# A decoder layer in fp32 pieces on one core: attention's product with the values from the last key block to the first, and the gating unit's scaling one tick later

## The chip, the cores and the metric

One core of a Trainium2 chip runs the whole layer as one program. The metric is device time of one execution in microseconds (us); lower is better. Engines are named as the profile names them: PE multiplies matrices, PEld loads PE's stationary operand, ACT and DVE work on elements, POOL does a little of that and issues some DMAs, SP issues the other DMAs.

## The reference, cut to what matters

One layer of a hybrid decoder: 512 tokens, width 2048. One projection gives the operands of two branches, a spatial gating unit and stick-breaking attention, whose merged result goes on into a feed-forward part and a per-layer embedding. The change lies in two places of the branches: the product of the attention weights with the values, and the norm of the gating unit's values.

```python
h = rmsnorm(x, attn_norm_g);  proj = h @ w_in        # u | v_sgu | q | k | v_att | g_a | g_b
...
v_sgu = rmsnorm(gelu(v_sgu).reshape(B, S, 8, 128), sgu_norm_g)
mixed = einsum('gts,bnsgc->bntgc', tril(w_s), v_sgu in chunks of 128) + b_s
y_a   = gelu(u) * mixed                              # gating unit
...
z      = einsum('bhqd,bhkd->bhqk', rmsnorm(q), rmsnorm(k)) * 128 ** -0.5    # 8 heads of 128
strict = key_pos < q_pos
log_1m = where(strict, log_sigmoid(-z), 0)
tail   = cumsum(log_1m, reverse=True) - log_1m       # sum over the keys behind this one
w      = where(strict, exp(log_sigmoid(z) + tail), 0)
y_b    = einsum('bhqk,bhkd->bhqd', w, v_att)         # <- the change's first part
...
x += (sigmoid(g_a) * (y_a @ w_up_a) + sigmoid(g_b) * (y_b @ w_up_b)) @ w_o
x += SwiGLU(rmsnorm(x));  x += sigmoid(rmsnorm(x) @ w_pg) * (p @ w_ple)
```

## The kernel before

**The large products.** The weights stream through the core in units: SP loads a unit into `wholes`, POOL issues a second load that adds onto it (L361), DVE adds two blocks (L373), and each unit is split into a high part on ACT (L357, into `whi`) and a low part on DVE (L354, into `wlo`), three slots of each in turn. A *pair* is one output block of 256 x 512 made of seven products of half-size blocks (a Strassen-like scheme) over eight units. Most products take three matmuls (L294, L295, L296: high by high, high by low, low by high); the first ones of many pairs, the *doubled* ones, take two (L683). When a pair's last unit is under way, its products end one after another in the `ps` banks of PSUM, and the *mix* puts them together: ACT copies halves of products out (L739), DVE adds and subtracts the others (L742). The next pair's products need the banks again, so a mix that ends late makes PE wait at the start of a product of the next pair. Two more banks of PSUM (`small`) serve everything else.

**The clock.** `tick()` is called while a pair adds its units: eight ticks a pair. Everything of the branches that is not a large product hangs on this clock: `beside(generator)` runs the generator on until its next `yield n`, and again n ticks later. So what lies between two yields is put into the instruction streams at one place among the pairs' matmuls; the engines then run their own streams in order. The scheduler may still move an instruction that is not ready in its model behind others, so that the place is not exactly that of the code; on ACT and DVE the weights' splits and the mix keep their order among each other (`in_turn`).

**Attention** runs in four rounds of two heads, between 120 and 560 us. A head has four key blocks of 128, j = 3 to 0; block j concerns the queries from block j on, (4 - j) * 128 columns. For each block, in the order j = 3, 2, 1, 0 (the `tail` is carried from behind), `stage_a` makes the scores (L1095), `stage_m` the masked logs, `stage_b` and `stage_c` split them (L1122 on ACT, L1126 on DVE), and `stage_d` makes the sums with a triangular matrix (L1132, L1133), subtracts them (L1137 on DVE) and takes the exponential (L1138 on ACT), which is the block's weights. `finish(h)` multiplies the four blocks with the values (L1145, plain fp32, which PE does as two passes) into one `small` bank, and ACT copies the result out (L1147). `finish(0)` stands after the second head's first `stage_b`, one tick behind the first head's last `stage_d`; `finish(1)` stands two ticks behind the second head's last `stage_d`.

**The gating unit** (`sgu_v`) runs in four calls of two halves, between 635 and 775 us. A half turns 512 tokens of one group over (L1021, PE), takes the squares' sums on ACT (L1028), scales and shifts them on DVE (L1193) and takes them to the power of -0.5 on POOL (L919, into `rr`). One `yield` later, ACT scales the values by `rr` (L1044, four times 128 columns; the same line serves attention's norms), and two yields later PE multiplies with the gating matrix (L1202, four matmuls of 128 columns), and DVE adds the bias (L1203).

The numbers behind names (`small_2849`) are a program's own count of buffers.

Of the kernel before, what the change touches and what calls it, by code (L numbers as in the profile page):

```python
# [19 lines left out]
P = 128  # L20
T = 512
NT = T // P
# [46 lines left out]
def hybrid_layer(  # L69
# [18 lines left out]
    nc = tc.nc  # L88
# [25 lines left out]
    class Arena:  # L114
# [28 lines left out]
        def give(self, block):  # L143
            self.turns += 1
            self.given[block.start // P : -(-(block.start + block.n) // P)] = self.turns
            holes = sorted(self.holes + [(block.start, block.n)])
            self.holes = holes[:1]
            for s, n in holes[1:]:
                if sum(self.holes[-1]) == s:
                    self.holes[-1] = (self.holes[-1][0], self.holes[-1][1] + n)  # L150
                else:
                    self.holes.append((s, n))
# [26 lines left out]
    def small_bank():  # L179
        return psa.tile([P, T], F32, tag="small", name=nm("small"))  # L180
# [333 lines left out]
    def load(src, n=1024, how="old"):  # L514
        b = take(n, how)
        nc.sync.dma_start(out=b.f(0, 1024), in_=src)
        return b
# [399 lines left out]
    def power(ms, n):  # L917
        r = rms_tile()[:, :n]
        nc.gpsimd.tensor_tensor(out=r, in0=ms, in1=expo[:, :n], op=ALU.pow)  # L919
        return r  # L920
# [90 lines left out]
    def a_tile(tag, n=T, start=0):  # L1011
        return att[tag].f(start, start + n)
# [4 lines left out]
    def flip(o):  # L1017

        ps = small_bank()
        for t in range(NT):  # L1020
            nc.tensor.transpose(ps[:, t * P : (t + 1) * P], o[:, t * P : (t + 1) * P], ident)  # L1021
        return ps

    def squares(ps):

        ms, junk = small(NT), tmp.tile([P, P], F32, tag="diag", name=nm("sq"))
        for t in range(NT):
            nc.scalar.activation(junk, ps[:, t * P : (t + 1) * P], AF.Square,  # L1028
                                 accum_out=ms[:, t : t + 1])
        return ms  # L1030
# [10 lines left out]
    def times(dst, ps, r):  # L1041
        for t in range(NT):
            s = slice(t * P, (t + 1) * P)
            nc.scalar.activation(dst[:, s], ps[:, s], AF.Copy, scale=r[:, t : t + 1])  # L1044
# [29 lines left out]
    def attention(rnd, kT, rk, v):  # L1074
        state = {}
# [64 lines left out]

        def finish(h):
            y = small_bank()
            for j in range(NT):
                c = h * T + j * P
                nc.tensor.matmul(y[:, j * P :], v[:, c : c + P], state.pop((h, "w", j)),  # L1145
                                 start=j == 0, stop=j == NT - 1)
            nc.scalar.activation(qT[:, h * T : (h + 1) * T], y, AF.Copy)  # L1147
            if h == 1:
                nc.sync.dma_start(out=y_spill[rnd], in_=qT)
                give(y_b[rnd])  # L1150
                y_done["b", rnd] = True
# [7 lines left out]
        for i, (h, j) in enumerate(blocks):  # L1159
            ahead = blocks[i + 1 : i + 3]  # L1160
            stage_b(j)
            yield 1
            if i == NT:
                finish(0)
            stage_c(j)
            if ahead:
                stage_m(*ahead[0])
            yield 1
            stage_d(h, j)
            if ahead[1:]:  # L1170
                stage_a(*ahead[1])
            yield 1
        yield 1
        finish(1)
        if rnd == 3:
            for tag in ("first", "k", "v", "zs", "zh", "zl"):
                give(att.pop(tag))

    def sgu_v(rnd, o):

        for h in range(2):
            g = 2 * rnd + h
            ws = a_tile("w2", P, rnd % 2 * P)
            nc.sync.dma_start(out=ws, in_=wsT[g])
            nc.gpsimd.affine_select(out=ws, in_=ws, pattern=[[1, P]], compare_op=ALU.is_ge,
                                    fill=0.0, base=0, channel_multiplier=-1)
            bb = a_tile("w1", P, rnd % 2 * P)
            nc.sync.dma_start(out=bb, in_=b_s[g : g + 1, :].broadcast_to([P, P]))
            yield 2
            gv = a_tile(("l", "w0")[rnd % 2])  # L1190
            ps = flip(o[:, h * T : (h + 1) * T])
            ssq = squares(ps)
            nc.vector.tensor_scalar(out=ssq, in0=ssq, scalar1=1.0 / P, scalar2=EPS,  # L1193
                                    op0=ALU.mult, op1=ALU.add)
            rr = power(ssq, NT)
            yield 1
            times(gv, ps, rr)
            yield 2
            mp = small_bank()
            for t in range(NT):  # L1200
                s = slice(t * P, (t + 1) * P)
                nc.tensor.matmul(mp[:, s], gv[:, s], ws, start=True, stop=True)  # L1202
            nc.vector.scalar_tensor_tensor(  # L1203
                out=o[:, h * T : (h + 1) * T].rearrange("p (n t) -> p n t", t=P),
                in0=mp.rearrange("p (n t) -> p n t", t=P),
                scalar=gcol[:, g_sgu + g : g_sgu + g + 1],
                in1=bb.unsqueeze(1).to_broadcast([P, NT, P]),
                op0=ALU.mult, op1=ALU.add)
# [78 lines left out]
    for n, ((w, i), pr) in enumerate(zip(order, made())):  # L1287
        if n == 0:
            row1 = norm1.row()
            for eps, c in ((eps_cols, EPS), (eps_q, EPS * P)):  # L1290
                nc.vector.tensor_scalar(out=eps, in0=norm1.mean, scalar1=c, scalar2=None,
                                        op0=ALU.mult)
        if n == 0:
            a_tiles()
        o = pr.out(block(w, i) if n < 3 else None)
        if w == "q":
            beside(q_prep(o, i))
        elif w == "k":
            kT, rk = o, rms_tile()
            beside(k_prep(kT, rk))  # L1300
            beside(attention(i, kT, rk, a_tile("v", 1024)), 6)
        elif w == "v":
            beside(v_prep(o, a_tile("v", 1024)))
        elif w == "s":
            scaled(o, row1)
            nc.scalar.activation(o, o, AF.Gelu_apprx_tanh)
            beside(sgu_v(i, o))
        elif w == "u":
            scaled(o, row1)
            nc.scalar.activation(o, o, AF.Gelu_apprx_tanh)  # L1310
            nc.vector.tensor_tensor(out=y_a[i].f(), in0=o, in1=y_a[i].f(), op=ALU.mult)
            y_done["a", i] = True
        else:
            d = tc.dram_tile([P, 1024], F32, name=nm("gsp"))
            nc.sync.dma_start(out=d, in_=o)
            gate_spill[w, i] = d
# [46 lines left out]
    for j in range(KU):  # L1363
# [10 lines left out]
        h = raw.popleft()  # L1374
# [41 lines left out]
    for c, units in enumerate(hs):  # L1416
# [3 lines left out]
        for j in range(KU):  # L1420
# [3 lines left out]
            h = load(spill["x1", j]) if end else None  # L1424
# [130 lines left out]
```

## Time and profile before

| | us |
|---|---|
| runs of the kernel (three) | 2667.51, 2673.37, 2673.16 |
| their median | 2673.16 |
| the profiled execution, its own time | 2668.2 |
| its span (first to last record) | 2666.5 |
| PE busy in the span | 2640.4 |
| DVE busy, ACT busy, POOL busy | 2236.4, 1413.9, 453.4 |
| granted TensorE clock (1 is full) | 0.998 |

The profile is one execution. The runs fall into two groups, one at 2667.5 to which the profiled execution belongs, the other 5.7 us above. "Busy" on PE includes time in which a matmul is in flight behind another. In the views, a row such as `288.98 2.39 PE L1145 MATMUL small<-wholes ... x8 [0.84 <-ACT wholes L1138]` reads: at 288.98 us PE began eight instructions of line 1145 that took 2.39 us together, and it had been idle for 0.84 us before, which ended when ACT's line 1138 had written `wholes`. fp32 matmuls are two instructions each in the trace, one for each pass.

### The profile page before, as it was taken

To read this page: it belongs to the slowest core of one execution; us is meant where nothing else is said; L and a number is where in the kernel's file an instruction comes from. 1 tells how busy PE (TensorE), PEld (TensorE's weight loads), DVE (VectorE), ACT (ScalarE), POOL (GpSimd) and SP (SyncE) were. 2 spreads that over 40 slices of the span, in tenths; PEclk is the share of its full clock that TensorE was granted. 3 is DMA by queue.
4 is the path that set the end of the run, shared out by engine and by line. 5 is a ranking of instruction groups with operands and counts; after the bars stand their busy time and mean duration, and the time that the engine had idled before them with its cause. 6 is when DMAs were issued, how large, how long until landed. Compare 5 with 4: busy or idle time off the path is not lost.

```text
span 2666.5 us, 42598 instructions
## 1 busy us (share of the span) xinstructions
PE 2640.4 (99%) x15354; PEld 2312.4 (87%) x15354; DVE 2236.4 (84%) x3791; ACT 1413.9 (53%) x2245; POOL 453.4 (17%) x557
## 2 busy tenths in 40 slices
PE   8999999999999999999999999999999999999999
PEld 7888898888998888888888888888888888889898
DVE  8687878787887658989889888888889989989876
ACT  7656565655554334576444444444445445455643
POOL 0222322222220001101111111111110211211010
PEclk9999999999999999999999999999999999999999
DMA  7577777677775669988888878888787989988884
GB/s 227 158 190 174 185 173 187 171 182 197 179 188 186 214 212 264 239 265 223 220 218 207 210 194 207 203 203 202 197 209 223 263 220 277 226 248 246 252 229 134
DMA packets 293875, 560.16 MB, mean 210 GB/s; under 512 B 26400, under 2 KB 140832, under 8 KB 293664
## 3 DMA queue, kind: packets, MB, share of 16 engines
q1 hardware_dynamic: 231408, 442.08, 50.4%
q0 software_dynamic: 62256, 115.37, 27.0%
q8 instruction: 120, 1.97, 0.3%
q14 instruction: 91, 0.75, 0.1%
HBM read 505.97 MB, written 51.38 MB: 209 GB/s over the span
## 4 chain that ended last, share of the span: by engine, by line
PE 88%; DVE 5%; ACT 2%; DMA 2%; issue 1%; POOL 0%; SPq 0%; POOLq 0%; DVEq 0%; ACTq 0%
PE ps L683 49%; PE ps L295 10%; PE ps L296 10%; PE ps L294 10%; PE small L683 6%; DVE wlo L354 2%; DVE out L742 1%; PE small L1145 1%; PE small L1021 1%; DMA wholes<-x 1%; DMA wholes<-w_in 1%; ACT whi L357 1%; DVE wholes L373 0%; PE small L1095 0%; DVE parts L285 0%
## 5 line engine op out<-in xcount | busy, mean ns | idle before, releaser
L683 PE MATMUL ps<-parts,whi 128*128 128x512 f32 x4200 | 1404.7, 398 | 3.7 <-DVE out L787 3.1
L357 ACT ACTIVATE whi<-wholes 128x512 fp32r<-128x512 f32 (+3 forms) x941 | 872.5, 940 | 727.6 <-DVE wholes L373 270.5
L354 DVE TENSOR_TENSOR wlo<-wholes,whi 128x512 fp32r<-128x512 f32 (+3 forms) x941 | 982.7, 1079 | 65.8 <-ACT whi L357 64.0
L683 PEld LDWEIGHTS ps<-parts,wlo 128*128 128x128 f32 x4200 | 788.9, 188 | 178.4 <-DVE wlo L354 1.1
L683 PE MATMUL ps<-parts,wlo 128*128 128x256 f32 x4200 | 832.0, 279 | 0.0
L683 PEld LDWEIGHTS ps<-parts,whi 128*128 128x128 f32 x4200 | 676.4, 189 | 10.2 <-issue 4.5
L294 PE MATMUL ps<-parts,whi 128*128 128x256 f32 (+1 forms) x1822 | 598.9, 330 | 8.0 <-ACT parts L284 5.6
L295 PE MATMUL ps<-parts,whi 128*128 128x256 f32 (+1 forms) x1838 | 605.9, 330 | 0.8 <-DVE parts L285 0.8
L296 PE MATMUL ps<-parts,wlo 128*128 128x256 f32 (+1 forms) x1838 | 605.8, 330 | 0.0
L295 PEld LDWEIGHTS ps<-parts,whi 128*128 128x128 f32 x1838 | 348.4, 190 | 39.0 <-DVE parts L285 2.4
L294 PEld LDWEIGHTS ps<-parts,whi 128*128 128x128 f32 x1822 | 344.6, 190 | 41.5 <-ACT parts L284 6.7
L296 PEld LDWEIGHTS ps<-parts,wlo 128*128 128x128 f32 x1838 | 348.8, 190 | 30.8
L373 DVE TENSOR_TENSOR wholes<-wholes 128x256 f32<-128x256 f32 x822 | 345.1, 420 | 21.7 <-DMA wholes<-w_ffn_in 2.6
L742 DVE TENSOR_TENSOR out<-out,ps 128x256 f32<-128x256 f32 x490 | 202.9, 416 | 149.9 <-ACT out L739 149.4
L361 POOL DMA_DIRECT2D wholes<-w_ffn_in x170 | 148.0, 870 | 691.2 <-DVE wholes L373 197.4
L361 POOL DMA_DIRECT2D wholes<-w_in x132 | 116.3, 882 | 523.1 <-DMA wholes<-w_in 146.8
L683 PE MATMUL small<-parts,whi 128*128 128x512 f32 x480 | 190.3, 396 | 0.0
L285 DVE TENSOR_TENSOR parts<-wholes,parts 128x1024 fp32r<-128x1024 f32 (+3 forms) x148 | 138.1, 945 | 23.0 <-ACT parts L284 23.0
L284 ACT ACTIVATE parts<-wholes 128x1024 fp32r<-128x1024 f32 (+3 forms) x148 | 119.3, 830 | 55.1 <-DVE wholes L525 33.3
L739 ACT ACTIVATE out<-ps 128x256 f32<-128x256 f32 x258 | 95.7, 382 | 49.9 <-PE ps L683 46.4
L361 POOL DMA_DIRECT2D wholes<-w_ffn_out x64 | 55.6, 869 | 358.3 <-DMA wholes<-w_ffn_out 136.5
L1395 ACT ACTIVATE out<-out 128x512 f32<-128x512 f32 x44 | 27.9, 634 | 159.2 <-DVE out L1394 159.2
(123 smaller groups left out, 1750.2 us busy)
## 6 DMA issues: line engine op xcount, KB each, us to landing
wholes<-w_ffn_in SPq DMA_DIRECT2D x170, 384.0 KB, 5.6
wholes<-w_in SPq DMA_DIRECT2D x132, 384.0 KB, 5.0
wholes<-w_ffn_in SPq DMA_DIRECT2D x170, 256.0 KB, 4.8
wholes<-w_ffn_in POOLq DMA_DIRECT2D x170, 256.0 KB, 5.4
wholes<-w_in SPq DMA_DIRECT2D x132, 256.0 KB, 4.0
wholes<-w_in POOLq DMA_DIRECT2D x132, 256.0 KB, 5.0
wholes<-w_ffn_out SPq DMA_DIRECT2D x64, 384.0 KB, 6.3
wholes<-x SPq DMA_DIRECT2D x45, 512.0 KB, 5.6
```

The costliest lines, as they stand in the source:

```text
L284: return (nc.scalar.activation(hi, src, AF.Copy), nc.vector.tensor_tensor(out=lo, in0=src, in1=hi.bitcast(F32), op=ALU.subtract))
L285: nc.vector.tensor_tensor(out=lo, in0=src, in1=hi.bitcast(F32), op=ALU.subtract))
L294: nc.tensor.matmul(ps, sh, mh, start=start, stop=False)
L295: nc.tensor.matmul(ps, sh, ml, start=False, stop=False)
L296: return nc.tensor.matmul(ps, sl, mh, start=False, stop=stop)
L354: in_turn(nc.vector.tensor_tensor(out=self.lo[:, blocks], in0=r, in1=h.bitcast(F32), op=ALU.subtract))
L357: in_turn(nc.scalar.activation(h, r, AF.Copy))
L361: nc.gpsimd.dma_start(out=raw[:, 3:5], in_=self.src[:, 1:3], accum_op=ALU.add)
L373: in_turn(nc.vector.tensor_tensor(out=o, in0=x, in1=y, op=ALU.add))
L683: m = nc.tensor.matmul(out, l, r, start=first and k == 0, stop=last and k == 1)
L739: in_turn(nc.scalar.activation(out, x, AF.Copy, scale=scale))
L742: in_turn(nc.vector.tensor_tensor(out=out, in0=x, in1=y, op=op))
```

## The change

Two edits. `finish` goes through the key blocks backwards, j = 3 to 0, so that the block whose weights are ready first is multiplied first. Block j alone touches the columns of query block j, and the blocks behind j have been summed already there; so each product is cut in two pieces, the columns behind the first 128, which are added to what the bank holds, and the first 128, which are new. For j = 3 there is the second piece only. A `finish` has 7 matmuls for 4, over the same 1280 columns; the bank is opened by the first and closed by the last of them. In `sgu_v` the scaling comes two ticks behind the power on POOL in place of one, and everything behind it in the half one tick later.

```diff
         def finish(h):
             y = small_bank()
-            for j in range(NT):
-                c = h * T + j * P
-                nc.tensor.matmul(y[:, j * P :], v[:, c : c + P], state.pop((h, "w", j)),
-                                 start=j == 0, stop=j == NT - 1)
+            for j in range(NT - 1, -1, -1):
+                c, w = h * T + j * P, state.pop((h, "w", j))
+                for a, b in ((P, (NT - j) * P), (0, P)):
+                    if a < b:
+                        nc.tensor.matmul(y[:, j * P + a : j * P + b], v[:, c : c + P], w[:, a:b],
+                                         start=j == NT - 1, stop=j + a == 0)
             nc.scalar.activation(qT[:, h * T : (h + 1) * T], y, AF.Copy)
...
             rr = power(ssq, NT)
-            yield 1
+            yield 2
             times(gv, ps, rr)
             yield 2
```

The added lines shift what stands below them by two: L1145, L1147, L1193, L1202 and L1203 are L1147, L1149, L1195, L1204 and L1205 in the changed kernel. ACT, DVE, POOL and SP have as many instructions as before; PE's program has 24 more (three in each of eight calls of `finish`). The orders differ in the attention rounds and in the gating unit's stage; behind the last half of the gating unit they are the same.

PE, the second round's `finish(0)`, between the last products of a pair (L683, their `ps` banks) and the second head's first sums (L1132). Before:

```order
L296 MATMUL ps_2734<-parts,wlo_81 128x256
L683 MATMUL ps_2691<-parts,whi_78 128x512
L683 MATMUL ps_2691<-parts,wlo_79 128x256 x2
L683 MATMUL ps_2691<-parts,whi_78 128x512
L683 MATMUL ps_2696<-parts,whi_78 128x512
L683 MATMUL ps_2696<-parts,wlo_79 128x256 x2
L683 MATMUL ps_2696<-parts,whi_78 128x512
L683 MATMUL ps_2701<-parts,whi_78 128x512
L1145 MATMUL small_2849<-wholes 128x512
L1145 MATMUL small_2849<-wholes 128x384
L1145 MATMUL small_2849<-wholes 128x256
L1145 MATMUL small_2849<-wholes 128x128
```

and now:

```order
L296 MATMUL ps_2740<-parts,wlo_81 128x256
L1147 MATMUL small_2855<-wholes 128x128 x3
L1147 MATMUL small_2855<-wholes 128x256
L1147 MATMUL small_2855<-wholes 128x128
L683 MATMUL ps_2697<-parts,whi_78 128x512
L1147 MATMUL small_2855<-wholes 128x384
L1147 MATMUL small_2855<-wholes 128x128
L683 MATMUL ps_2697<-parts,wlo_79 128x256 x2
```

Five of the seven pieces, those of the key blocks 3, 2 and 1, stand ahead of the product's first matmul; the two of key block 0 stand one matmul behind it, where all four stood nine matmuls (of L683) behind the same point.

ACT at the same place: the exponential of key block 0 (L1138, 512 columns), the copies of the mix (L739) and of the result (L1147, now L1149). Before:

```order
L1100 ACTIVATE wholes<-wholes 128x256
L357 ACTIVATE whi_80<-wholes 128x1280
L1138 ACTIVATE wholes<-wholes 128x512
L739 ACTIVATE out_2867<-ps_2691 128x256
L739 ACTIVATE out_2867<-ps_2696 128x256
L1147 ACTIVATE wholes<-small_2849 128x512
L739 ACTIVATE out_2867<-ps_2701 128x256
```

and now:

```order
L1100 ACTIVATE wholes<-wholes 128x256
L357 ACTIVATE whi_80<-wholes 128x1280
L1138 ACTIVATE wholes<-wholes 128x512
L1149 ACTIVATE wholes<-small_2855 128x512
L739 ACTIVATE out_2876<-ps_2697 128x256
L739 ACTIVATE out_2876<-ps_2702 128x256
L739 ACTIVATE out_2876<-ps_2707 128x256
```

What stands ahead of the exponential is as it was; the result's copy went ahead of two copies of the mix.

DVE at the first half of the gating unit, the bias (L1203, now L1205) among a pair's mix (L742) and the splits (L354). Before:

```order
L1203 SCALAR_TENSOR_TENSOR wholes<-small_6499,gcol,wholes 128x512
L742 TENSOR_TENSOR wholes<-wholes,ps_6352 128x256
L742 TENSOR_TENSOR wholes<-wholes,ps_6357 128x256
L742 TENSOR_TENSOR wholes<-wholes 128x256
L742 TENSOR_TENSOR wholes<-wholes,ps_6362 128x256
L354 TENSOR_TENSOR wlo_79<-wholes,whi_78 128x1280
L354 TENSOR_TENSOR wlo_79<-wholes,whi_78 128x512
L742 TENSOR_TENSOR wholes<-wholes 128x256
L742 TENSOR_TENSOR p_644_6515<-p_644_6515,ps_6373 128x256
```

and now:

```order
L742 TENSOR_TENSOR wholes<-wholes,ps_6386 128x256
L354 TENSOR_TENSOR wlo_79<-wholes,whi_78 128x1280
L354 TENSOR_TENSOR wlo_79<-wholes,whi_78 128x512
L742 TENSOR_TENSOR wholes<-wholes 128x256
L742 TENSOR_TENSOR p_642_6530<-p_642_6530,ps_6397 128x256
L1205 SCALAR_TENSOR_TENSOR wholes<-small_6559,gcol,wholes 128x512
L742 TENSOR_TENSOR wholes<-wholes,ps_6405 128x256
L742 TENSOR_TENSOR wholes<-wholes,p_642_6530 128x2x256
```

The bias went from ahead of the mix into its middle, ahead of the mix's last four instructions. On PE, the half's matmuls (L1202, now L1204) stand sixteen matmuls of L683, four products of the ending pair, later.

## The prediction

> **What bounds the kernel now.** I read the head of the page first, then the chain of waits, the windows by stage, and the waits of PE in the stretch that the change touches.
>
> ```profile
> span 2666.5 us, 42598 instructions
> PE 2640.4 (99%) x15354; PEld 2312.4 (87%) x15354; DVE 2236.4 (84%) x3791; ACT 1413.9 (53%) x2245; POOL 453.4 (17%) x557
> PE 88%; DVE 5%; ACT 2%; DMA 2%; issue 1%; POOL 0%; SPq 0%; POOLq 0%; DVEq 0%; ACTq 0%
> ```
>
> PE is busy for 99% of the span, and the chain that ends last is PE's for 88%. So a gain can only be a gap of PE that closes or matmul time that goes. By stage:
>
> ```profile
> 140.00:620.00 480.00, 473.90 (x2992) 419.61 (x2992) 391.15 (x705) 293.29 (x611) 127.98 (x181) 1.00 0.72 183
> 620.00:760.00 140.00, 138.97 (x926) 126.94 (x925) 114.56 (x190) 82.43 (x172) 35.41 (x39) 1.00 0.73 180
> 760.00:2667.00 1907.00, 1895.20 (x10772) 1654.59 (x10769) 1629.08 (x2708) 937.77 (x1263) 270.51 (x306) 1.00 0.80 220
> ```
>
> The second column is the stretch, the third PE's busy time. Attention (140 to 620 us) leaves 480.00 - 473.90 = 6.1 us of PE idle, most of the gating unit's stage (620 to 760) 1.0 us. Behind 760 us the instructions stand in the old order, so nothing is to be had there but a shift of the whole. What the idle time in the two stages waits for:
>
> ```profile
> PE small L1145 <- ACT wholes L1138: 2.5, 3, 0.8
> PE small L1133 <- DVE parts L1126: 1.6, 4, 0.7
> PE small L1095 <- ACT wholes L1044: 1.2, 3, 0.4
> PE small L1202 <- ACT wholes L1044: 1.0, 1, 1.0
> PE small L1145 <- issue: 0.8, 1, 0.8
> ```
>
> The columns are total, times, longest. The rows that the change can reach are the first, the fourth and the last: four waits at `finish(0)`, 2.5 + 0.8 = 3.3 us, and one at the gating unit, 1.0 us. Together 4.3 us, 0.16% of the span. Nothing in the two edits can make the kernel faster by more than about that, and what a measurement of this kernel can tell from no change is 0.3%, 8 us. The question is rather what they may cost.
>
> **The price of a split.** A product of 512 columns becomes one of 384 and one of 128, and so on: 3 matmuls more in each of 8 calls, in two passes each, 48 more on PE over the same columns. The second round's `finish(0)`, with what stands around it, on PE, ACT and DVE:
>
> ```profile
> 286.33 0.40 PE L683 MATMUL ps<-parts,whi 128*128 128x512 f32 x1
> 287.51 0.62 PE L683 MATMUL ps<-parts,whi 128*128 128x512 f32 x2
> 288.98 2.39 PE L1145 MATMUL small<-wholes 128*128 128x512 f32 x8 [0.84 <-ACT wholes L1138]
> 291.13 0.48 PE L683 MATMUL ps<-parts,wlo 128*128 128x256 f32 x2
> 292.37 0.22 PE L1132 MATMUL small<-parts,tri 128*128 128x128 f32 x1
> 287.06 1.26 ACT L357 ACTIVATE whi<-wholes 128x1280 fp32r<-128x1280 f32 x1
> 288.22 0.61 ACT L1138 ACTIVATE wholes<-wholes 128x512 f32<-128x512 f32 x1
> 288.74 0.63 ACT L739 ACTIVATE out<-ps 128x256 f32<-128x256 f32 x2
> 291.41 0.60 ACT L1147 ACTIVATE wholes<-small 128x512 f32<-128x512 f32 x1 [2.04 <-PE small L1145]
> 286.03 0.67 DVE L1137 TENSOR_TENSOR wholes<-wholes,small 128x512 f32<-128x512 f32 x1
> 291.19 0.42 DVE L1104 SCALAR_TENSOR_TENSOR wholes<-wholes 128x256 f32<-128x256 f32 x1 [0.84 <-PE small L1145]
> ```
>
> From the start of the eight L1145 to that of the next L683, 291.13 - 288.98 = 2.15 us for 2 x 1280 columns, 0.84 ns a column. The only other plain fp32 matmuls in a row that are all 128 wide are those of the gating unit:
>
> ```profile
> 661.38 1.05 PE L1202 MATMUL small<-wholes 128*128 128x128 f32 x8
> 662.27 0.60 PE L1021 MATMUL small<-ident,wholes 128*128 128x128 f32 x4
> ```
>
> 662.27 - 661.38 = 0.89 us for 8 x 128 columns, 0.11 us each, where 128 columns at 0.84 ns are 0.108. So a matmul of its own costs 3 or 4 ns beyond its columns: 48 x 3.5 ns = 0.17 us. Below, the bound is 0, since the columns stay; above, each of the 48 takes a slot of 0.11 us beyond its columns: 5.3 us. I take **+0.15 us**: the row is of the same kind, type and width, and each with a weight load of its own.
>
> The Trainium skill speaks against the split: "TensorE: Matmul & The Clock Gate", section "Back-to-back issue gap", says that in a stream of weight load and matmul, one of 128 columns takes 81 ns where it alone would take 56, as the load adds to it. By that page 48 x 25 ns = 1.2 us would be an estimate of the cost; the row above, with its loads, has no such excess.
>
> **`finish(0)`, four times.** Its first matmul before takes the weights of key block 0, the last that come. They are the exponential L1138 of 288.22 to 288.83. PE, through with its seven slots of L683 (0.235 us each, from 286.33), is ready at 287.98 and starts at 288.98: a gap of 1.0 us, of which the profile shows 0.84 as idle. Now the five pieces of key blocks 3, 2 and 1 come first, whose weights have long been there: 2 x 768 columns x 0.84 ns = 1.29 us, from 286.33 to 287.62; then one slot of L683, to 287.86. There the pieces of block 0 stand and need the same L1138. It is where it was: ahead of it on ACT stand the same instructions, up to the split L357 of 1280 columns (287.06 to 288.32), and its DVE operand (L1137) was done at 286.70. So PE waits from 287.86 to 288.98, 1.1 us for 1.0. What stood ahead of the wait as filling, seven slots of L683, has been exchanged for the pieces and one slot. Then the two pieces, 2 x 512 columns, 0.86 us, to 289.84, and the eleven slots left, 11 x 0.235 = 2.58, to 292.42, where the next L1132 started at 292.37. The wait stays, because it is set by ACT and not by the order of PE: +0.05 us, with the start of an L1147 behind a product's matmul perhaps +0.1 a round; four rounds, **+0.3 us** with the split's share set apart.
>
> What else moves there: the result's copy L1147 goes ahead of the mix's copies on ACT, and waits for block 0's pieces, to 290.1 or so. The mix's first copy then starts some 1.9 us later than at 288.74, but its product now ends later too, and the third copy, which started at 291.90, stays within 0.2 us. That is hidden by the time until the next pair needs the bank that the mix ends last. DVE's L1104, which waited 0.84 us behind the product, now has its operand and goes earlier; DVE is not what PE waits for there. The bounds for the four: -4 us (each gap of 1.0 closes), +4 us (each mix is late by as much). `finish(1)` shows no wait before:
>
> ```profile
> 187.26 2.32 PE L1145 MATMUL small<-wholes 128*128 128x512 f32 x8
> ```
>
> No bracket, so there is nothing to gain, and its order changes nothing but the split.
>
> **The gating unit, eight halves.** The first, on ACT, POOL, PE and DVE:
>
> ```profile
> 646.74 1.14 ACT L1044 ACTIVATE wholes<-small,rr 128x128 f32<-128x128 f32 x4 [3.05 <-POOL rr L919]
> 647.75 1.29 ACT L357 ACTIVATE whi<-wholes 128x1280 fp32r<-128x1280 f32 x1
> 644.77 0.86 POOL L361 DMA_DIRECT2D wholes<-w_in  x1 [1.24 <-DVE wlo L354]
> 645.33 1.37 POOL L919 TENSOR_TENSOR rr<-ms,expo 128x4 f32<-128x4 f32 x1
> 645.85 0.28 PE L296 MATMUL ps<-parts,wlo 128*128 128x256 f32 x1
> 647.16 1.26 PE L1202 MATMUL small<-wholes 128*128 128x128 f32 x8 [1.03 <-ACT wholes L1044]
> 648.17 0.47 PE L683 MATMUL ps<-parts,whi 128*128 128x512 f32 x1
> 648.46 0.75 DVE L1203 SCALAR_TENSOR_TENSOR wholes<-small,gcol,wholes 128x512 f32<-128x512 f32 x1 [3.11 <-PE small L1202]
> 649.57 0.42 DVE L742 TENSOR_TENSOR wholes<-wholes,ps 128x256 f32<-128x256 f32 x1 [0.36 <-ACT wholes L739]
> 650.28 0.42 DVE L742 TENSOR_TENSOR wholes<-wholes,ps 128x256 f32<-128x256 f32 x1 [0.29 <-ACT wholes L739]
> 655.46 0.68 DVE L742 TENSOR_TENSOR wholes<-ps,wholes 128x512 f32<-128x512 f32 x1
> 657.13 0.28 PE L294 MATMUL ps<-parts,whi 128*128 128x256 f32 x1
> ```
>
> The power on POOL (645.33 to 646.70) stands behind an accumulating load; ACT idles 3.05 us for it, and PE, ready at 645.97, starts L1202 at 647.16: 1.19 us lost. The changed order puts the matmuls four products later, so PE does not wait: -1.19. But ACT's scaling comes out no later: two of the four L1044 still stand ahead of the split of 1280 columns and wait for the same `rr`. So ACT is free for the mix only at 649.0, while PE's products now begin at 645.97 instead of 648.17; the mix is held by ACT, not by PE. On DVE, the bias leaves the place ahead of the mix and stands before its last four instructions, where it takes 0.65 us of the engine. ACT's first copy comes 0.15 us sooner than 649.15, when the mix's first L742 at 649.57 could have it, and the wait of 0.29 for the next one closes: the last L742 ends at 656.14 - 0.15 - 0.29 + 0.65 = 656.35. PE wants that bank at 657.13 - 1.19 = 655.94, and waits 0.4 us. Net **-0.8 us**.
>
> At the next two halves ACT's burst (squares, scalings behind two powers, two splits) is longer by a second wait for POOL, whose power takes 1.4 us as above, half of it behind other work: an estimate of 0.7 us by which the mix's copies come later.
>
> ```profile
> 677.90 0.68 DVE L742 TENSOR_TENSOR out<-ps,out 128x512 f32<-128x512 f32 x1
> 678.50 0.42 DVE L373 TENSOR_TENSOR wholes<-wholes 128x256 f32<-128x256 f32 x1
> 679.54 0.28 PE L294 MATMUL ps<-parts,whi 128*128 128x256 f32 x1
> ```
>
> The last L742 ends at 678.58, 0.96 us ahead of PE. With 0.7 us of ACT and about 0.5 of the bias in the mix it ends near 679.75, and PE comes at 678.8 (0.8 earlier, by the first half): **+0.95 us**. In the other halves the matmuls went behind the mix's products, which start 0.86 us earlier for it and pay for the bias: 0. Sum of the stage +0.15; bounds -1.2 (nothing is late) and +3 (the three halves' mixes each a microsecond late). POOL and SP issue the same DMAs; two small loads of the gating matrix go ahead of a weight load in SP's queue, and weights lie ready for microseconds, so I set that at 0.
>
> **The sum.** 0.15 + 0.3 + 0.15 = +0.6 us on the profiled execution's 2668.2 (span 2666.5): 2668.8. The median of the runs stands 5.0 us above that execution, with one of the three below it; so the runs' own two groups are wider apart than any term, and the same sum on the median gives 2673.8. I forecast no change and name a time between, **2671 us**. The likeliest case lies in 2663 (the lower bounds together, -5.2, on the faster group) to 2676 (about a third of the upper ones, +7.2, on the slower).
>
> **The rivals.**
>
> A: the backward order does close the gaps at `finish(0)`. If ACT reaches L1138 a microsecond sooner than I read, or the five pieces hide it, 4 x 1.0 us go and the gating unit's 1.2 with them: 2668.2 - 5.2 = 2663.0, on the median 2668. For it: four waits are for exactly this operand. Against it: the exponential is last by either order, and the filling is exchanged, not added. Chance 0.13; nearly all of it is still within 0.3%.
>
> B, slower: ACT, held by the power behind POOL's accumulating load, makes the mix late in every half. Its place is the last L742 of a mix and the next pair's product in that bank; it decides once the mix is later than the 0.96 us of the rows above. Price: the ACT idle of 3.05 us less about 1.0 of slack, eight times, 16.4, less 1.2 at the first half: 2668.2 + 15.2 = 2683.4. For it: the scaling and its split now stand nearer to the mix. Against it: of the eight powers, one alone made PE wait before, and the weights' splits have room. Chance 0.11.
>
> C: each of the 48 pieces costs a slot, as if two passes with own weight loads did not overlap: +5.3, 2673.5 on the profiled execution. Against it: the row of eight at 0.11 us each. Chance 0.07.
>
> That leaves 0.69 for the forecast. **Faster** by over 0.3% would need all of the 4.3 us and more, 0.04; **slower** is B and a bad C, 0.13; the rest, 0.83, within 0.3%. The range, 2662 to 2682, takes the likeliest case, A and C, and reaches up to near B.
>
> **What would show it.** L1147 in the changed kernel still waits for L1138 about four times, at the pieces of key block 0, 0.8 us or so each: then the finish term is right; no such wait, then A. From the last piece to the next L683 some 0.86 us behind the start of block 0's pieces, and 2.15 us for all seven: then the split is right; 2.8 us or more, then C. The wait of L1204 is gone, and in its place PE waits at L294 for a DVE L742 once or twice, under 1 us each; more than three such waits of over 1 us are B. The forecast is wrong if PE's idle time between 140 and 760 us moves by more than 4 us, or the busy time behind 760 us changes at all.

## The result, and the profile after

The changed kernel is a little slower: median 2678.68 us of 22 runs beside 2671.32 us of 22 runs of the kernel before, ratio 1.0024 with a 95% interval of 1.0017 to 1.0031, 6.4 us (4.5 to 8.3). One of the changed kernel's runs took 3703.88 us at a granted clock of 0.655; it is left out of the ratio, which compares the other runs and not the two medians. The time lies in the range that was given and inside the 0.3%, but it is not the "no change" of the forecast: the interval leaves out 1. Run once more beside other runs of the kernel before, the ratio was 1.0029 (1.0015 to 1.0043). The changed kernel's profiled execution took 2678.85 us. The 22 runs of the kernel before lie all along from 2667.34 to 2673.87 us, so the two groups that three runs suggested, between which 2671 us was named, are not there.

The page of the changed kernel, its head and the chain by engine:

```profile
span 2677.2 us, 42703 instructions
PE 2643.6 (99%) x15402; PEld 2317.3 (87%) x15402; DVE 2233.1 (83%) x3791; ACT 1412.9 (53%) x2245; POOL 458.6 (17%) x557
PE 80%; DVE 8%; DMA 5%; ACT 3%; issue 2%; POOL 1%; SPq 0%; ACTq 0%; POOLq 0%; DVEq 0%
```

PE has the 48 matmuls more and only 3.2 us more of busy time, while the span is 10.7 us longer: the rest, 7.5 us, is idle time. The windows of the two stages:

```profile
140.00:620.00 480.00, 473.39 (x3032) 422.90 (x3031) 388.60 (x703) 294.37 (x611) 130.05 (x180) 1.00 0.74 182
620.00:760.00 140.00, 137.40 (x909) 124.80 (x909) 112.66 (x189) 80.39 (x171) 37.77 (x39) 1.00 0.74 179
```

and what PE waits for between 140 and 760 us (total, times, longest):

```profile
PE small L1147 <- ACT wholes L1138: 3.3, 4, 0.8
PE small L1133 <- DVE parts L1126: 2.2, 4, 1.2
PE small L1204 <- ACT wholes L1044: 2.0, 2, 1.1
PE small L1095 <- ACT wholes L1044: 1.1, 3, 0.4
PE ps L683 <- DVE wholes L742: 0.6, 1, 0.6
```

Attention has its four waits for L1138 as before (3.3 us, where 2.5 and 0.8 stood). The gating unit, which lost 1.0 us once, now loses 2.0 us by 760 us, and a third such wait of 0.9 us lies behind.

To see where time goes, one thing helps: the 14,890 large matmuls (L294 to L296, L291, L683) are the same in the same order in every kernel here, so the start of each can be compared with its start in the first profile of before. The changed kernel's come 0.25 us earlier at 100 us, 0.46 later at 620, 3.82 later at 790, and 10.63 later at 2600. In the table below, *attention* is what is added from 100 to 620 us, *gating* from 620 to 790, *behind* from 790 to 2600; each from one profiled execution.

| kernel | ratio to before (95%) | attention | gating | behind |
|---|---|---|---|---|
| before again (c0_before) | 0.9998 (0.9990 to 1.0007) | +0.8 | -1.0 | +1.4 |
| **the change** | 1.0024 (1.0017 to 1.0031) | +0.7 | +3.4 | +6.8 |
| the change again (c1_after) | 1.0029 (1.0015 to 1.0043) | +0.3 | +5.8 | +4.7 |
| finish edit (e1_finish) | 1.0008 (0.9999 to 1.0018) | +1.0 | +0.3 | +4.5 |
| finish edit again (c2_finish) | 1.0014 (1.0005 to 1.0022) | +1.5 | +0.7 | +2.6 |
| gating edit (e2_yield) | 1.0020 (1.0011 to 1.0029) | +0.9 | +3.6 | +3.5 |
| second half a tick later (e3) | 1.0047 (1.0029 to 1.0065) | +0.6 | +10.7 | -3.2 |
| scaling alone later (e4) | 1.0001 (0.9990 to 1.0012) | +0.1 | +2.8 | +2.3 |
| gating edit, second half's start kept (e5) | 0.9999 (0.9989 to 1.0009) | +0.1 | 0.0 | -0.2 |
| the change, second half's start kept (e10_mended) | 1.0006 (0.9997 to 1.0015) | -0.1 | +0.8 | +5.8 |
| the same again (c3_mended) | 1.0007 (0.9997 to 1.0016) | +1.2 | -0.7 | +1.4 |
| split, old order (e7) | 1.0007 (0.9998 to 1.0016) | +0.3 | -1.0 | +1.6 |
| 24 passes added (e8_pad) | 1.0009 (0.9999 to 1.0019) | +2.8 | +1.4 | +2.0 |
| first head's product a tick later (e6) | 0.9987 (0.9978 to 0.9995) | -3.4 | +0.4 | +0.6 |
| e6 and e5 (e9_both) | 0.9983 (0.9973 to 0.9992) | -3.9 | -1.5 | +4.3 |
| finish edit, key block 0 a tick later (e11) | 0.9991 (0.9982 to 0.9999) | -3.2 | -0.7 | +5.4 |
| **e11 and e5 (e12_both)** | 0.9987 (0.9978 to 0.9996) | -3.3 | -0.6 | -1.1 |

Now the place that I had set at nothing: the second half of the gating unit's third call. Before, on PE and ACT:

```profile
717.77 0.60 PE L1021 MATMUL small<-ident,wholes 128*128 128x128 f32 x4
725.96 1.05 PE L1202 MATMUL small<-wholes 128*128 128x128 f32 x8
718.41 0.28 ACT L1028 ACTIVATE sq<-small 128x128 f32<-128x128 f32 x1
722.48 1.06 ACT L1310 ACTIVATE out<-out 128x1024 f32<-128x1024 f32 x1 [2.50 <-DVE out L1212]
723.45 1.78 ACT L357 ACTIVATE whi<-wholes 128x512 fp32r<-128x512 f32 x2
725.13 1.12 ACT L1044 ACTIVATE wholes<-small,rr 128x128 f32<-128x128 f32 x4
```

and in the changed kernel on PE, ACT, DVE and POOL:

```profile
721.85 0.60 PE L1021 MATMUL small<-ident,wholes 128*128 128x128 f32 x4
733.22 1.26 PE L1204 MATMUL small<-wholes 128*128 128x128 f32 x8 [0.87 <-ACT wholes L1044]
723.28 1.06 ACT L1312 ACTIVATE out<-out 128x1024 f32<-128x1024 f32 x1 [3.60 <-DVE out L1214]
724.25 1.78 ACT L357 ACTIVATE whi<-wholes 128x512 fp32r<-128x512 f32 x2
725.93 0.25 ACT L1028 ACTIVATE sq<-small 128x128 f32<-128x128 f32 x1
732.80 1.14 ACT L1044 ACTIVATE wholes<-small,rr 128x128 f32<-128x128 f32 x4 [2.79 <-POOL rr L919]
728.83 0.16 DVE L1195 TENSOR_SCALAR ms<-ms 128x4 f32<-128x4 f32 x1
729.56 0.86 POOL L361 DMA_DIRECT2D wholes<-w_in  x1 [5.34 <-DVE ms L1195]
730.12 2.64 POOL L919 TENSOR_TENSOR rr<-ms,expo 128x4 f32<-128x4 f32 x1
```

The transposes (L1021) went to the other side of a pair's end, and with them the squares (L1028) went on ACT from ahead of the Gelu of the pair's result (L1310, now L1312) to behind it. That Gelu waits for DVE, and two splits follow: the squares start 4.08 us behind the transposes (725.93 - 721.85), where it was 0.64. The power then ends at 732.76, and the scaling at 732.80 is what PE waits for. From the transposes to L1204 it takes 11.4 us, where it was 8.2. The code's distance grew by one tick only. The squares pass a Gelu like this in all four second halves of the changed kernel, and PE waits in three of them: those of the first, third and fourth call.

### The profile page after: what moved, and what is told of

It reads as the page before. It is cut to its first block, busy times and chain, and to the rows that moved or that the text cites. A ratio compares the mean times of both kernels' runs of the same rounds, so it can differ in the third digit from the quotient of the medians.

```text
span 2677.2 us, 42703 instructions
## 1 busy us (share of the span) xinstructions
PE 2643.6 (99%) x15402; PEld 2317.3 (87%) x15402; DVE 2233.1 (83%) x3791; ACT 1412.9 (53%) x2245; POOL 458.6 (17%) x557
## 4 chain that ended last, share of the span: by engine, by line
PE 80%; DVE 8%; DMA 5%; ACT 3%; issue 2%; POOL 1%; SPq 0%; ACTq 0%; POOLq 0%; DVEq 0%
PE ps L683 46%; PE ps L295 9%; PE ps L296 9%; PE ps L294 9%; PE small L683 6%; DVE wlo L354 3%; DVE out L742 2%; ACT whi L357 1%; DMA wholes<-w_ffn_out 1%; DMA wholes<-mix 1%; DVE wholes L373 1%; DMA wholes<-w_in 1%; PE small L1021 1%; PE small L1147 0%; ACT parts L284 0%
## 5 line engine op out<-in xcount | busy, mean ns | idle before, releaser
L683 PE MATMUL ps<-parts,whi 128*128 128x512 f32 x4200 | 1408.1, 398 | 6.6 <-DVE out L787 4.8
L354 DVE TENSOR_TENSOR wlo<-wholes,whi 128x512 fp32r<-128x512 f32 (+3 forms) x941 | 981.7, 1077 | 73.0 <-ACT whi L357 72.1
L683 PEld LDWEIGHTS ps<-parts,wlo 128*128 128x128 f32 x4200 | 789.8, 188 | 178.3 <-DVE wlo L354 1.1
L683 PE MATMUL ps<-parts,wlo 128*128 128x256 f32 x4200 | 832.2, 279 | 0.0
L683 PEld LDWEIGHTS ps<-parts,whi 128*128 128x128 f32 x4200 | 677.8, 189 | 13.8 <-issue 7.8
L294 PE MATMUL ps<-parts,whi 128*128 128x256 f32 (+1 forms) x1822 | 598.7, 330 | 8.7 <-ACT parts L284 5.4
L296 PE MATMUL ps<-parts,wlo 128*128 128x256 f32 (+1 forms) x1838 | 605.9, 331 | 1.0 <-DVE wlo L354 0.9
L294 PEld LDWEIGHTS ps<-parts,whi 128*128 128x128 f32 x1822 | 344.7, 190 | 41.6 <-ACT parts L284 6.3
L296 PEld LDWEIGHTS ps<-parts,wlo 128*128 128x128 f32 x1838 | 348.9, 190 | 33.4 <-DVE wlo L354 2.4
L373 DVE TENSOR_TENSOR wholes<-wholes 128x256 f32<-128x256 f32 x822 | 344.4, 419 | 20.3 <-DVE wlo L354 3.0
L742 DVE TENSOR_TENSOR out<-out,ps 128x256 f32<-128x256 f32 x490 | 202.4, 415 | 160.5 <-ACT out L739 160.2
L361 POOL DMA_DIRECT2D wholes<-w_ffn_in x170 | 148.2, 872 | 691.8 <-DMA wholes<-w_ffn_in 221.4
L361 POOL DMA_DIRECT2D wholes<-w_in x132 | 116.7, 885 | 518.0 <-DMA wholes<-w_in 139.2
L683 PE MATMUL small<-parts,whi 128*128 128x512 f32 x480 | 190.3, 397 | 0.0
L739 ACT ACTIVATE out<-ps 128x256 f32<-128x256 f32 x258 | 96.6, 385 | 47.9 <-PE ps L683 44.4
L361 POOL DMA_DIRECT2D wholes<-w_ffn_out x64 | 55.7, 870 | 354.8 <-DMA wholes<-w_ffn_out 148.9
```

What stands on the lines that cost most here:

```text
L294: nc.tensor.matmul(ps, sh, mh, start=start, stop=False)
L296: return nc.tensor.matmul(ps, sl, mh, start=False, stop=stop)
L354: in_turn(nc.vector.tensor_tensor(out=self.lo[:, blocks], in0=r, in1=h.bitcast(F32), op=ALU.subtract))
L361: nc.gpsimd.dma_start(out=raw[:, 3:5], in_=self.src[:, 1:3], accum_op=ALU.add)
L373: in_turn(nc.vector.tensor_tensor(out=o, in0=x, in1=y, op=ALU.add))
L683: m = nc.tensor.matmul(out, l, r, start=first and k == 0, stop=last and k == 1)
```

## The experiments

**How much an unchanged kernel moves.**

> The kernel before, once more, as a measure of what an unchanged program varies by. Ratio 1.000. If the time that the changed profile lost behind 780 us (6.8 of its 10.6 us, in four places of unchanged order: 1047, 1175, 2287 and 2507 us) is what executions differ by, this profile also moves by some microseconds against the first one at the same places; if it is a consequence of the change, this profile agrees with the first one within 1 us there.

Measured: ratio 0.9998; within 1.4 us of the first profile in each stage. The gating stage's -1.0 is the first half's wait, which this execution did not have: the power on POOL began sooner there, since the load ahead of it was issued sooner. So of the changed kernel's 10.6 us, the gating stage's 3.4 are beyond what this shows, and so, by this one comparison, are the 6.8 behind it.

**The two edits apart.** The diff of the first is the change's part in `finish`, of the second the change of `yield 1` to `yield 2`.

> The finish edit alone (backward order, split products), the gating unit as before. My theory: four waits for L1138 as before, the split nearly free, so between 140 and 620 us PE's matmuls come 0 to 1 us later than before, and the gating stage is as before: ratio 1.000, at most +1 us. Rival C (a slot of 0.11 us for each piece): +5 us. Rival A (the waits close): -4 us.

> The gating unit's edit alone. Theory: it carries nearly all of the loss. In the stage the first half wins 1.2 us and the second halves of three calls lose 1.2 to 1.3 us each at L1202, so that the matmuls behind 780 us come 2.5 to 4 us later than before; ratio 1.001 to 1.003. Rival: the loss is shared with the finish edit, ratio under 1.001.

Measured: the gating edit alone 1.0020 (1.0011 to 1.0029), with +3.6 us in its stage; the finish edit alone 1.0008, with +1.0 in attention (0.8 in the unchanged kernel's second profile). The theory holds in the main: the gating edit carries most. Rivals A and C of the finish edit fall.

**What in the gating edit.** Its tick moves three things: the scaling, the matmuls behind it, and the start of the second half. In the first kernel the second half alone starts a tick later; in the next, the scaling alone is later; in the last, scaling and matmuls are later, but the second half starts where it did.

```diff
 # e3_second_half, at the end of a half
+            if h == 0:
+                yield 1
 # e4_scale_only
-            yield 1
-            times(gv, ps, rr)
             yield 2
+            times(gv, ps, rr)
+            yield 1
 # e5_start_kept (and e10, c3: the same on the changed kernel)
-            yield 2
+            yield 2 - h
             gv = a_tile(("l", "w0")[rnd % 2])
...
-            yield 1
+            yield 2
             times(gv, ps, rr)
```

> The scaling's tick as before, but the second half of each call starts one tick later, as it does in the changed kernel as a consequence. Theory (what costs is where the second half's transposes and squares fall, just behind a pair's end, where ACT has two more splits and a Gelu ahead of the squares): the power then comes as late as in the changed kernel, while the matmuls stand a tick (1.7 us) sooner, so each second half loses about 2 to 3 us: +6 to +12 us, ratio 1.002 to 1.0045; the first half keeps its old wait of 1.0 us. Rival (what costs is the scaling's own tick): within 1 us of before in the stage, ratio 1.000.

> The scaling one tick later, but the matmuls behind it and the second half where they were (the second wait is one tick instead of two). Theory (the loss comes from where the second half falls, not from the scaling's tick): the gating stage as before within 1 us, with the first half's wait of about 1 us still there, ratio 1.000. Rival (the later scaling itself is what makes L1202 wait): waits of 1 us or more at the second halves, +3 us or more, ratio over 1.001.

> The scaling a tick later and the matmuls too, as in the change, but the second half of a call starts a tick after the first half's matmuls instead of two, so that its transposes stand at the old tick. Theory: no wait at L1202 in any second half, the first half's wait gone; PE's matmuls behind 780 us come 0 to 1.2 us sooner than before; ratio 0.9995 to 1.000. Rival (the second halves wait wherever they start, because their matmuls stand in a mix): +3.5 us as with the gating unit's edit alone.

Measured: e3 1.0047, +10.7 us in the stage. Its third call's second half, on ACT and PE:

```profile
726.01 1.07 ACT L1312 ACTIVATE out<-out 128x1024 f32<-128x1024 f32 x1 [4.03 <-DVE out L1214]
728.66 0.26 ACT L1028 ACTIVATE sq<-small 128x128 f32<-128x128 f32 x1
735.73 1.14 ACT L1044 ACTIVATE wholes<-small,rr 128x128 f32<-128x128 f32 x4 [3.41 <-POOL rr L919]
736.15 2.08 PE L1202 MATMUL small<-wholes 128*128 128x128 f32 x8 [3.35 <-ACT wholes L1044]
```

The squares are behind the Gelu again, without any change to the scaling's own tick, and PE, which gets to the matmuls a tick sooner, waits 3.35 us. In e5 the order is the old one, squares at 718.77 ahead of the Gelu at 722.45:

```profile
718.77 0.28 ACT L1028 ACTIVATE sq<-small 128x128 f32<-128x128 f32 x1
722.45 1.06 ACT L1310 ACTIVATE out<-out 128x1024 f32<-128x1024 f32 x1 [2.10 <-DVE out L1212]
725.10 1.13 ACT L1044 ACTIVATE wholes<-small,rr 128x128 f32<-128x128 f32 x4
```

There is no wait at L1202 in any half, the stage adds 0.0 us, and the ratio is 0.9999. The first half's wait is gone as well, but not for a gain: PE waits 0.8 us for a mix (L683 for DVE's L742) soon after. e4 has a ratio of 1.0001 and no wait at L1202 in the second halves; my figure for its first half was off, 2.1 us for "about 1", since two of the four L1044 went behind the split of 1280 columns there, and its profile has +2.8 in the stage. The runs do not show that as a loss, though their interval would hold one of 3 us. e5, with the same tick at the scaling, adds 0.0 us in the stage. So the start of the second half is the cause, not the scaling's tick.

> The changed kernel once more. Theory: the gating stage loses the same 3 to 3.5 us between 620 and 780 us as in its first profile, with waits at L1204 in second halves; what it lost behind 780 us (6.8 us there) need not come back at the same size, since kernels with nothing changed there moved by 0 to 3 us at the same places. Ratio 1.002 to 1.003. Rival (the loss behind 780 us belongs to the change): 6 us or more behind 780 us again.

> The changed kernel with one thing put back: the second half of a call starts one tick behind the first half's matmuls instead of two, at the tick it had before. Theory: no wait at L1204 in a second half, the gating stage within 1 us of before, ratio 1.0003 to 1.001 (what is left is the finish edit's). Rival (the finish edit and the gating edit lose together in another way): ratio stays over 1.0015.

> The mended kernel, once more, for the same question: with a late loss that goes with the backward order 4 us or more behind 780 us and a ratio of 1.0012 or more; otherwise any size from -3 to 7 us there and a ratio of 1.0000 to 1.0008.

Measured: the change again 1.0029, with waits at L1204 of 4.5 us in four places and +5.8 in the stage, more than the theory's 3.5: in this execution the fourth half lost too. With the second half's start put back, 1.0006 and 1.0007, the stage at +0.8 and -0.7, and no second half waits at L1204 (the first half of one does in e10, 0.9 us). That one line takes back some 4.7 us (1.0024 less 1.00065) of the change's 6.4, a rough figure, since each ratio is known to about 2 us. What is left, some 1.7 us, is not explained by the gating unit.

**The split.**

```diff
             for j in range(NT):
-                c = h * T + j * P
-                nc.tensor.matmul(y[:, j * P :], v[:, c : c + P], state.pop((h, "w", j)),
-                                 start=j == 0, stop=j == NT - 1)
+                c, w = h * T + j * P, state.pop((h, "w", j))
+                for a, b in ((P, (NT - j) * P), (0, P)):
+                    if a < b:
+                        nc.tensor.matmul(y[:, j * P + a : j * P + b], v[:, c : c + P], w[:, a:b],
+                                         start=j == 0 and a == P, stop=j == NT - 1)
```

> The products split in the same seven pieces, but from the first key block to the last as before. It prices the split by itself. Theory: seven pieces take 2.2 us from the first to the matmul behind them where four took 2.15, so 8 x 0.02 to 0.05 us: within 0.5 us at 620 us. Rival C: 0.66 us each time, +5 us at 620 us.

Measured: +0.3 us in attention, ratio 1.0007 (0.9998 to 1.0016). A whole `finish(1)` in the changed kernel, fourteen passes and what follows:

```profile
186.89 2.35 PE L1147 MATMUL small<-wholes 128*128 128x128 f32 x14
189.00 0.48 PE L683 MATMUL ps<-parts,whi 128*128 128x512 f32 x1
```

189.00 - 186.89 = 2.11 us for 1280 columns in two passes, where eight passes took 2.08 (189.34 - 187.26 in the profile of before). Eight times 0.03 is 0.24 us. Rival C is out.

**A bare delay.** In e8 the last half's four matmuls are done four times over.

```diff
-            for t in range(NT):
-                s = slice(t * P, (t + 1) * P)
+            for t in range(NT * (4 if g == 7 else 1)):
+                s = slice(t % NT * P, (t % NT + 1) * P)
```

> The kernel before with the last half's four matmuls (L1202, the eighth half) done four times over: 24 more passes of 0.11 us, 2.6 us more on PE at 769 us, nothing else changed. It asks what a bare delay of about the size of the gating unit's loss becomes by the end. Theory: a delay stays what it is, +2.6 us at 780 us and +2.6 in the median (ratio 1.001). Rival: the loads behind 1000 us answer to the shift, and a delay of 2.6 us costs 5 or more at the end, in the profile at 1047 and 1175 us and in the median (ratio 1.002).

Measured: 2.7 us where it stands, ratio 1.0009 (0.9999 to 1.0019), that is 2.4 us (-0.3 to 5.1). The profile adds 2.0 us behind. The runs fit a delay that stays what it is; their interval does not exclude the rival, and neither does the profile, with 2.7 + 2.0 = 4.7 us.

**The loss behind 790 us.**

> The finish edit alone, once more. If the backward order makes the late loss, the profile loses 4 us or more behind 780 us again, and the median is 4 us or more over before (ratio 1.0015 or more). If it is the execution that differs, the profile may lose anything from -3 to 7 us there, and the ratio stays at 1.0003 to 1.0010.

Measured: 2.6 us behind, ratio 1.0014 (1.0005 to 1.0022). This lies between the two forecasts. Together with c3 (+1.4 with the backward order), e9 (+4.3 without it) and e12 (-1.1 with it), the loss behind does not come with the backward order every time: one program gave +5.8 and +1.4. In the changed kernel's first profile it falls at two places above all, 2.8 us each: at 1047 us, where PE's first products with `w_o` wait for a bank that DVE's L787 has to empty, and at 1175 us, where a later product waits for ACT's L873 (1.0 us of this comes back by 1205). Before and after, from PE's waits behind 760 us:

```profile
PE ps L683 <- DVE out L787: 3.1, 1, 3.1
PE ps L294 <- ACT out L873: 0.6, 1, 0.6
```

```profile
PE ps L683 <- DVE out L787: 4.8, 1, 4.8
PE ps L294 <- ACT out L873: 1.8, 1, 1.8
```

The waits grow by 1.7 and 1.2 us only; the rest of each 2.8 goes into the matmuls right behind the wait, which start further apart than before.

At the first place DVE is late because it waits for a block that was stored to DRAM and is loaded again (L516, `mix`), and SP issues the first of three such loads sooner or later against PE: in six of the seventeen other profiles 1.0 to 2.1 us later than in the first, and all six lose 2.6 to 4.2 us there; of the other eleven, where it comes up to 1.6 us sooner, one loses 1.9 and none else more than 1.1. This is one way in which executions of one kernel can come to differ by several microseconds (2662 to 2677 us for the kernel before, over all runs here). The second place was not followed further. Whether the finish edit makes the late case more frequent is open, but the profiles point that way: of the eight with the backward order five are late at the first place and six lose 2 us or more at the second; of the other ten, one and two. Its two ratios, 1.0008 and 1.0014, are 2 to 4 us, and attention itself shows no more than the 0.1 to 2.8 us that kernels with the old `finish` show there.

**Can the waits for L1138 be had?** In e6 the first head's whole product comes a tick later, unsplit; there the second head's masked logs of key block 2 are written first into the place of the first head's weights, so the kernel multiplies with those: the amount of work is the same, that block's values are not. In e9 the gating edit of e5 comes in as well. In e11 and e12 the backward order is kept, and key block 0 alone, whose weights are not overwritten, comes a tick later.

```diff
 # e11_block0_later, on the finish edit (product = its loop over the blocks js)
             if i == NT:
-                finish(0)
+                y = small_bank()
+                product(y, 0, range(NT - 1, 0, -1))
             stage_c(j)
             if ahead:
                 stage_m(*ahead[0])
             yield 1
+            if i == NT:
+                finish(0, y)      # product(y, 0, (0,)) and the copy
             stage_d(h, j)
```

> The kernel before with the first head's product with the values one tick later, behind the second head's masked logs, in the old order and unsplit. It asks whether the four waits of 1.0 us for L1138 can be had. Theory: PE reaches the product some 1.2 us later and the weights are there: no wait at L1145, 4 us less at 620 us, ratio 0.9985 (0.998 to 0.9995). Rival: the wait goes over to the next thing of attention, L1132 or L1133, which then wait longer, ratio 1.000.

> The later product of the first head and the gating unit's edit with the second half's start kept, together, on the kernel before. Theory: the product's 4 us and nothing from the gating unit but the first half's wait, 0 to 1 us: ratio 0.998 to 0.9995. Rival: as for the run with the later product alone, ratio 1.000.

> The finish edit alone, and in the first head's product the two pieces of key block 0 one tick behind the other five. Theory: the wait belongs to key block 0's weights alone, and a tick (1.7 us) is more than the 1.0 us that they are late, so no wait for L1138 is left and PE's matmuls come 3.5 to 4 us sooner at 620 us than with the finish edit alone; ratio to before 0.9985 to 0.9995. Rival: the wait goes over to L1132 or L1133 behind it, 0 us, ratio as with the finish edit alone, 1.0008.

> The mended kernel (whole change, with the second half's start kept) with key block 0's pieces one tick later, as in the run before. Theory: 3.5 to 4 us under the mended kernel, ratio to before 0.9985 to 0.9995. Rival: as the mended kernel, 1.0006.

Measured: attention takes 3.2 to 3.9 us less in all four, and the ratios are 0.9987, 0.9983, 0.9991 and 0.9987, the last with an interval of 0.9978 to 0.9996. e11's second round on PE:

```profile
283.73 1.49 PE L1146 MATMUL small<-wholes 128*128 128x128 f32 x10
284.97 0.47 PE L683 MATMUL ps<-parts,whi 128*128 128x512 f32 x1
...
287.85 1.03 PE L1146 MATMUL small<-wholes 128*128 128x384 f32 x4
288.63 0.31 PE L1132 MATMUL small<-parts,tri 128*128 128x128 f32 x1
```

and all that PE waits for in e12 between 140 and 760 us:

```profile
PE small L1133 <- DVE parts L1126: 1.1, 4, 0.4
PE small L1095 <- ACT wholes L1044: 1.1, 3, 0.4
PE ps L683 <- DVE wholes L742: 0.6, 1, 0.6
```

No bracket at L1146, and no wait has come up elsewhere in its place. e12, which leaves nothing out, is 0.13% (0.04 to 0.22) under before.

## Why the prediction was wrong, point by point

**The bound on the gain** was right: attention's four waits and the gating unit's one were all that could be had, and e12 took 3.3 us of the 4.3 there.

**The split**, +0.15 us: 0.24 measured. That is 5 ns for each of the 48. By the Trainium skill's figures ("TensorE: Matmul & The Clock Gate", section "Back-to-back issue gap") an estimate is 25 ns; this trace, with 5 ns, does not agree for plain fp32.

**`finish(0)`**, "the wait stays, because it is set by ACT and not by the order of PE": right, to the row. The changed kernel's second round on PE and ACT:

```profile
286.22 1.49 PE L1147 MATMUL small<-wholes 128*128 128x128 f32 x10
287.47 0.48 PE L683 MATMUL ps<-parts,whi 128*128 128x512 f32 x1
288.77 1.13 PE L1147 MATMUL small<-wholes 128*128 128x384 f32 x4 [0.82 <-ACT wholes L1138]
289.66 0.48 PE L683 MATMUL ps<-parts,wlo 128*128 128x256 f32 x2
288.11 0.61 ACT L1138 ACTIVATE wholes<-wholes 128x512 f32<-128x512 f32 x1
289.94 0.60 ACT L1149 ACTIVATE wholes<-small 128x512 f32<-128x512 f32 x1 [1.22 <-PE small L1147]
```

The five early pieces take 1.25 us (1.29 was worked out), one slot of L683 follows, and PE waits for the same L1138, which ends where it ended. The filling was exchanged. The finish edit's two ratios are 2 to 4 us, where the sum had 0.45; in its profiles the rest lies behind 790 us, where the sum had no term, and its cause is open. Rival A needed something more to put in its place, which e11 gave.

**The first half of the gating unit**, -0.8 us: the matmuls of the pair behind it come 0.08 us sooner than before where they came 0.46 later at 620 us, so -0.5. ACT did hold the mix: PE waits 0.6 us for its L742, at L683, where 0.4 at L294 was worked out.

**The next two halves**, +0.95 us by a late bank at L294: about +1.3 there, near in size, but it was not that bank. PE waited at L1204 for the scaling.

**The other halves, "0"**: this is the step that failed. It looked at where the matmuls L1204 went, and took their scaling to be early enough. It counted one tick between the power and the scaling, and did not follow what the generator does with it: `sgu_v` does its halves one behind the other, so the first half's tick also puts the second half's transposes and squares a tick later, past a pair's end, and behind the Gelu and two splits on ACT. The second halves of the third and fourth call lose 1.25 us each in the first profile; in the second one all four second halves do. The gating term was +0.15 us; it measured +3.4 and +5.8, and 3.6 with that edit alone. With the second half's start put back it is 0.0, +0.8 and -0.7.

The squares' place makes the scaling late; how late, and so whether PE waits, depends on POOL too. In the second call's second half the first profile has the power at 687.45, for 1.28 us, and PE does not wait. In the second profile PE and the squares come 1.5 us sooner, but the load ahead of the power (L361) is issued at 687.23 after 6.36 us of waiting for DVE's L373, the power begins at 687.79 and takes 1.73 us, and PE waits 1.3 us.

**Rival B** had a link of this chain, POOL's power behind an accumulating load, and the wrong end: the costly wait was at L1204, not at a mix, and in the second halves alone.

**The test behind 760 us** (wrong if "the busy time behind 760 us changes at all") was too strict: the same program moves by some microseconds there from execution to execution. PE's idle time between 140 and 760 us went from 7.1 to 9.2 us, within the 4 us that were allowed. The sign that did tell was "the wait of L1204 is gone": there are three of them, 2.9 us in all.

## What to carry to other kernels

Where work is hung on a clock between other work, a tick added in one step moves every step behind it in the same routine, the next round's too. List each of them on its own engine, and ask what it passes: here the costly move was of four squares past one Gelu that itself waits. And an order that puts the late operand last gains only if the part that needs it may come later too.

## What was not expected of the hardware

POOL's power of 128 x 4 elements took from 1.04 to 2.36 us in the first profile of before and up to 2.93 in its second (POOL's spans are rough); with a load ahead of it, as in the second call above, it decides whether the scaling is in time. And the same load of `mix` was issued, against PE, from 1.6 us sooner to 2.1 us later than in the first profile; where it was late, PE lost 2.6 to 4.2 us.
